# A two-layer hybrid block on one core: the first stage takes its tokens as columns, and two weight sums are made by adding transfers

## The chip, the core and the metric

One core of one Trainium2 chip runs the whole program. The metric is device time in microseconds, the median of three runs. The engines are TensorE (PE; its weight loads are PEld), VectorE (DVE), ScalarE (ACT), GpSimd (POOL) and SyncE (SP, which only issues transfers). Transfers issued by SP or by POOL are carried by the core's 16 DMA engines.

## The reference

256 tokens of width 1024 go through six sublayers, each followed by a residual and a layer norm. Four of them are feed-forward layers (2816 hidden features), one is a mixer of a gated delta rule and a state-space scan (hybrid), one is sparse attention.

```
def swiglu(x, w_in, w_out):
    gate, up = jnp.split(x @ w_in, 2, axis=-1)
    return (jax.nn.silu(gate) * up) @ w_out
...
        h = layer_norm(DEEPNORM_ALPHA * h + 0.5 * swiglu(h, ffn_w_in[layer, 0], ffn_w_out[layer, 0]),
                       ln_g[layer, 0], ln_b[layer, 0])
```

The mixers enter in the same way with the factor 1.

## The kernel before

**Arithmetic.** All arrays are float32. Every factor is split in two, hi (the value rounded to the matmul's format, made by ACT's copy) and lo (the rest, made by DVE as value minus hi), and a product is three matmuls: hi by hi, hi by lo, lo by hi. So each 512 KB weight tile (128 x 1024) is loaded as `raw`, cast by ACT to `whi` and subtracted by DVE to `wlo` (`halved`, line 676), and then used by PE. Tokens stand as columns, `x`, split in the same way; `X` is a copy that isn't split.

**Stages.** The order is feed-forward, hybrid, feed-forward, feed-forward, attention, feed-forward. A feed-forward stage (`ffn`, line 1044) makes its 22 tiles of 128 hidden features in three ways: four by products per block of tokens, two by column products, and the last 16 in four chunks of four by `wide` (line 751). In a chunk the 2 x 2 blocks of w_in (gate and up, two halves of the depth) meet seven combined forms of x (`token_forms`): seven products named a to g, twelve matmuls each, instead of eight. Four weight blocks of two tiles, b11, b12, b21 and b22, are loaded; products b, d, e and f need sums of blocks, which DVE adds in place: b is b11 + b12, d is that + b22, e is b12 + b22, f is (the sum of d) + b21. Each hidden tile then meets a tile of w_out in twelve matmuls (a term) into four PSUM banks, `acc`; `TERMS` says how many terms follow each of a chunk's products. `rows` (line 705) loads the w_out tiles; for the seven in `ADDED` of each stage lo is made by ACT as minus the rounded tile, to which a transfer that POOL issues adds the tile from memory.

**Start.** `run` (line 2103) loads x's rows in four pieces of 256 KB into `h`; PE turns them by transposes against `ident`, and ACT and DVE copy and split the result out of PSUM (`transpose_half`). `first_steps` and `first_weights` (lines 1011 and 717) load the gate and the up tiles, four each, and multiply them with both token blocks. Matmuls of `ones` (`spin`) keep PE at work before and between.

**Order.** The program is recorded and then put in order by a planner (`order`, line 352), which picks for each engine the operation that can start first by its own costs, and by program order among those that can start now. Each engine runs its list in that order and waits at the first operation that isn't ready. All operations carry line 561 in the profile, where the list is written out, so groups are told apart by tile names. SBUF has 52 tiles of 4 KB a partition (`m4`) for all of this.

Of the kernel before, what the change touches and what calls it, by code (L numbers as in the profile page):

```python
# [18 lines left out]
P = 128  # L19
# [3 lines left out]
DFF = 2816  # L23
# [27 lines left out]
CHUNKS, AHEAD, LAG = 4, 3, 7  # L51

TERMS = ((0, 1, 1, 1, 1, 1, 1), (0, 0, 1, 1, 1, 1, 0), (0, 0, 1, 1, 1, 1, 0), (0, 0, 1, 1, 1, 0, 0))

ADDED = range(8, 22, 2)
# [6 lines left out]
RANK = 0  # L62

# [118 lines left out]
class Op:  # L182
    __slots__ = ("eng", "fn", "args", "kw", "idx", "prio", "cost", "table", "deps", "succ", "ndep", "ready", "start",
                 "end", "alloc", "dense", "alts", "tiles", "nbytes", "quad", "port", "banks")


class Plan:
# [11 lines left out]
    def __init__(self):  # L199
        self.ops = []  # L200
        self.tiles = []
        self.base = 0
        self.gate = None
        for e in ("tensor", "vector", "scalar", "gpsimd", "sync"):
            setattr(self, e, _Eng(self, e))
# [7 lines left out]
    def add(self, eng, fn, args, kw, alts=None):  # L213
# [3 lines left out]
        op.alts = alts  # L217
        op.deps, op.succ, op.alloc, op.nbytes = {}, [], None, 0
# [133 lines left out]
    def order(self, caps):  # L352
# [95 lines left out]
        while left:  # L448
            best = None
            for e in engs:  # L450
# [6 lines left out]
                for op in lst:  # L457
# [16 lines left out]
                    key = (st if st > f + 1e-9 else f, p)  # L474
                    if cand is None or key < cand[0]:
                        cand = (key, op, pen)
# [5 lines left out]
            (key, op, pen), e = best  # L482
            st = key[0] + pen
# [101 lines left out]
class K:  # L585
    NT = 2
# [130 lines left out]
    def first_weights(self, w, n0, arrivals):  # L717

        out = []
        for n in range(4):  # L720
            src = w[n0 + n]
            raw = self.m4(1024, "raw", "W")
            hi, lo = (self.m4(1024, name, "W", F32R) for name in ("whi", "wlo"))
            step = 512 if arrivals and n < 2 else 1024
            for e in range(0, 1024, step):
                cs = slice(e, e + step)
                self.nc.sync.dma_start(raw[:, cs], src[:, cs])
                self.split(hi[:, cs], lo[:, cs], raw[:, cs])
                for f in (arrivals.pop(0) if arrivals else []):
                    f()  # L730
            out += [(hi[:, k * 512:k * 512 + 512], lo[:, k * 512:k * 512 + 512]) for k in range(2)]
        return out
# [18 lines left out]
    def wide(self, w, n0, forms, gout):  # L751
# [31 lines left out]
        add(b11, b12)  # L783
# [3 lines left out]
        add(b11, b22)  # L787
        product(r, "d", b11, False, False)
        nc.scalar.activation(t, r, AF.Copy)
        yield  # L790
        add(b12, b22)
# [6 lines left out]
        yield  # L798
        b21 = load(3)
        p = self.bank("ps")  # L800
# [1438 lines left out]
```

## Time and profile before

| | |
|---|---|
| median of three runs | 1086.62 us (1086.55 to 1088.65) |
| the profiled execution's own time | 1087.19 us |
| its span, first to last instruction | 1085.5 us |
| idle time of PE in the span, 1085.5 - 1066.3 | 19.2 us |
| mean DMA rate over the span | 199 GB/s |
| bytes moved | 215.71 MB |
| granted PE clock, mean | 0.995 |

A row of a group reads: line, engine, operation, output <- inputs, sizes, count, then its busy time and the mean of one in ns. A row of the timeline reads: start and length in us, engine, line, operation, and in brackets the idle time before it and what ended it. The granted clock is TensorE's, as a share of full speed.

### The profile page before, as it was taken

What the parts mean: (1) busy time and instruction counts of PE and PEld (TensorE: products, weight loads), DVE (VectorE), ACT (ScalarE), POOL (GpSimd) and SP (SyncE); (2) the same over time, 40 slices, a digit from 0 to 9 for tenths busy, and PEclk for the clock granted to TensorE, in tenths of its full rate; (3) what the DMA queues carried; (4) which work ended last, traced back from release to release, by engine and by line L of the source; (5) the groups of instructions that cost most, each with busy time, mean ns of one, the idle gap of its engine ahead of it and who ended that gap; (6) DMA issues with size and microseconds to landing.
All of it is one profiled execution on the core that took longest, in us unless ns stands there. A gap on an engine that the chain in (4) does not pass through costs nothing.

```text
span 1085.5 us, 16212 instructions
## 1 busy us (share of the span) xinstructions
PE 1066.3 (98%) x5946; PEld 893.3 (82%) x5946; DVE 1010.9 (93%) x1453; ACT 725.9 (67%) x1155; POOL 70.7 (7%) x116
## 2 busy tenths in 40 slices
PE   8999999998999999999999999999999999999997
PEld 6788888897999788888888888888887778888886
DVE  7999999799979999999999999999978889999995
ACT  7767866368737774667866667678465778666780
POOL 1000000001001310000000000000001000000000
PEclk9999999999999999999999999999999899999999
DMA  8658768535433575367777736679563336457881
GB/s 330 231 196 256 221 233 284 179 135 182 140 115 99 194 269 180 117 230 251 215 229 254 257 125 215 235 241 303 189 214 98 92 123 216 152 188 236 255 231 41
DMA packets 65034, 215.71 MB, mean 199 GB/s; under 512 B 8301, under 2 KB 12218, under 8 KB 64954
## 3 DMA queue, kind: packets, MB, share of 16 engines
q1 hardware_dynamic: 60922, 199.98, 52.8%
q0 software_dynamic: 4032, 14.68, 7.2%
q8 instruction: 47, 0.77, 0.3%
q14 instruction: 33, 0.27, 0.1%
HBM read 211.86 MB, written 1.07 MB: 196 GB/s over the span
## 4 chain that ended last, share of the span: by engine, by line
PE 84%; DVE 12%; ACT 1%; DMA 1%; issue 1%; POOL 0%; SPq 0%; DVEq 0%; ACTq 0%
PE ps L561 39%; PE acc L561 31%; PE mp L561 14%; DVE wlo L561 2%; DVE cv L561 2%; DVE arena L561 1%; DMA raw<-in_ffn_w_in_dram 1%; DVE o L561 1%; DVE sw L561 1%; DVE x L561 1%; DVE y L561 1%; DVE qs L561 1%; DVE AT L561 0%; POOL arena L561 0%; DVE Y L561 0%
## 5 line engine op out<-in xcount | busy, mean ns | idle before, releaser
L561 ACT ACTIVATE whi<-raw 128x1024 fp32r<-128x1024 f32 (+1 forms) x435 | 436.8, 1052 | 104.0 <-DVE raw L561 85.4
L561 DVE TENSOR_TENSOR wlo<-raw,whi 128x1024 fp32r<-128x1024 f32 (+2 forms) x419 | 491.4, 1205 | 7.1 <-ACT whi L561 6.1
L561 PE MATMUL ps<-whi,x 128*128 128x512 f32 (+1 forms) x864 | 234.8, 390 | 0.3 <-ACT cv L561 0.3
L561 PEld LDWEIGHTS ps<-whi,x 128*128 128x128 f32 x864 | 156.7, 188 | 30.6 <-issue 1.5
L561 DVE TENSOR_TENSOR raw<-raw,raw 128x1024 f32<-128x1024 f32 x128 | 152.8, 1216 | 0.0
L561 PE MATMUL ps<-wlo,x 128*128 128x512 f32 (+1 forms) x432 | 127.1, 385 | 0.0
L561 PE MATMUL ps<-x,whi 128*128 128x256 f32 (+2 forms) x560 | 114.3, 312 | 4.0 <-ACT cv L561 2.4
L561 PEld LDWEIGHTS ps<-x,whi 128*128 128x128 f32 (+1 forms) x560 | 90.4, 188 | 11.4 <-ACT cv L561 3.8
L561 PE MATMUL acc<-whi,gh 128*128 128x512 f32 x253 | 99.3, 393 | 0.0
L561 PE MATMUL acc<-wlo,gh 128*128 128x512 f32 x253 | 99.0, 391 | 0.0
L561 PE MATMUL acc<-whi,gl 128*128 128x512 f32 x253 | 97.9, 390 | 0.0
L561 PEld LDWEIGHTS ps<-wlo,x 128*128 128x128 f32 x432 | 79.6, 188 | 15.3 <-issue 0.4
L561 PE MATMUL ps<-x,wlo 128*128 128x256 f32 (+1 forms) x344 | 80.0, 284 | 0.5 <-DVE wlo L561 0.5
L561 PE MATMUL acc<-whi,x 128*128 128x512 f32 x224 | 73.7, 405 | 2.3 <-DVE x L561 0.8
L561 PE MATMUL acc<-whi,g 128*128 128x512 f32 x192 | 63.3, 392 | 0.0
L561 POOL DMA_DIRECT2D wlo<-in_ffn_w_out_dram x28 | 24.4, 872 | 569.2 <-ACT wlo L561 391.3
L561 PEld LDWEIGHTS ps<-x,wlo 128*128 128x128 f32 (+1 forms) x344 | 58.1, 189 | 2.1 <-DVE wlo L561 0.7
L561 PEld LDWEIGHTS acc<-whi,gl 128*128 128x128 f32 x253 | 47.5, 188 | 9.8
L561 PEld LDWEIGHTS acc<-whi,gh 128*128 128x128 f32 x253 | 47.5, 188 | 9.5
L561 PEld LDWEIGHTS acc<-wlo,gh 128*128 128x128 f32 x253 | 47.5, 188 | 9.5
L561 PEld LDWEIGHTS acc<-whi,x 128*128 128x128 f32 x224 | 41.8, 189 | 11.8 <-ACT whi L561 2.1
L561 PE MATMUL mp<-whi,fhi 128*128 128x512 f32 x128 | 49.9, 390 | 0.0
(284 smaller groups left out, 1735.2 us busy)
## 6 DMA issues: line engine op xcount, KB each, us to landing
raw<-in_ffn_w_in_dram SPq DMA_DIRECT2D x174, 512.0 KB, 5.5
raw<-in_ffn_w_out_dram SPq DMA_DIRECT2D x88, 512.0 KB, 3.7
wlo<-in_ffn_w_out_dram POOLq DMA_DIRECT2D x28, 512.0 KB, 8.5
raw<-in_hyb_w_col_dram SPq DMA_DIRECT2D x28, 512.0 KB, 4.5
raw<-in_hyb_w_tok_dram SPq DMA_DIRECT2D x16, 512.0 KB, 7.8
raw<-in_hyb_w_out_dram SPq DMA_DIRECT2D x16, 512.0 KB, 3.7
raw<-in_nsa_w_tok_dram SPq DMA_DIRECT2D x8, 512.0 KB, 6.6
raw<-in_nsa_w_one_dram SPq DMA_DIRECT2D x8, 512.0 KB, 5.8
```

The costliest lines, as they stand in the source:

```text
L561: r = getattr(getattr(nc, eng), fn)(*[res(a) for a in args], **{k: res(a) for k, a in kw.items()})
```

## The change

**The start.** The host lays x out a second time as columns (`x_cols`: four pieces of 128 x 512, two depth tiles of both token blocks each). `first_loads` issues these between the weight tiles, straight into `X`, and all 16 transposes and their copies out of PSUM go: ACT and DVE split `X` as it lies in SBUF. The rows of x are still needed for the first residual and are now loaded behind the first stage's weights. The matmuls of `ones` all stand ahead.

```diff
-    def first_weights(self, w, n0, arrivals):
+    def first_loads(self, x, w):
+        raws = []
+        for n in range(8):
+            if n < 4:
+                nc.sync.dma_start(x[1][n // 2][:, :, n % 2 * 2:n % 2 * 2 + 2, :],
+                                  self.i['x_cols'][n].rearrange("p (b k t) -> p b k t", b=2, k=2))
             raw = self.m4(1024, "raw", "W")
+            for cs in [slice(0, 512), slice(512, 1024)] if n == 0 else [slice(0, 1024)]:
+                nc.sync.dma_start(raw[:, cs], w[n][:, cs])
+            raws.append(raw)
+        return raws
...
+                if c0 == 0:
+                    hi, lo = (x[0][n][:, :, e] for e in range(2))
+                    self.split(hi, lo, x[1][n // 2][:, :, n % 2 * 2:n % 2 * 2 + 2, :].rearrange("p b k t -> p k b t"))
...
+            with self.late():
+                nc.sync.dma_start(self.ah[b], self.i['x'][0, b * P:(b + 1) * P])
...
-        spin(4, 2)
+        spin(4, 4)
...
-        load(0, 0)
-        with _Gate(self.plan, len(self.plan.ops) - 3):
-            spin(2, 2)
```

**The sums.** The sums of e and f are made by adding transfers that POOL issues, two tiles each in each of 16 chunks; those of b and d stay on DVE. No w_out tile is made by a transfer any more. Product c moves from the sixth place in a chunk to the second, behind a.

```diff
-ADDED = range(8, 22, 2)
+ADDED, EARLY = (), 3
+SUMS = ("e", "f")
...
-        def add(out, a):
+        def add(name, out, a, block):
             for e in range(2):
-                V.tensor_tensor(out[e], out[e], a[e], OP.add)
+                if name in SUMS:
+                    nc.gpsimd.dma_start(out[e], w[n0 + 2 * block + e], accum_op=OP.add)
+                else:
+                    V.tensor_tensor(out[e], out[e], a[e], OP.add)
...
         b12 = load(1)
-        add(b11, b12)
+        add("b", b11, b12, 1)
+        if "e" in SUMS:
+            add("e", b12, None, 2)
+        b21 = load(3)
+        p = self.bank("ps")
+        product(p, "c", b21, True, True)
...
         product(r, "d", b11, False, False)
+        if "f" in SUMS:
+            add("f", b11, None, 3)
...
-        b21 = load(3)
-        p = self.bank("ps")
-        product(p, "c", b21, True, True)
```

**The planner.** Operations of a layer norm count as able to start 135 ns sooner on DVE and ACT when the next one is picked. Constants for a variant with five chunks come in as well, but all four stages keep four.

```diff
-                    key = (st if st > f + 1e-9 else f, p)
+                    at = st - HOT if op.hot and e in ("vector", "scalar") else st
+                    key = (at if at > f + 1e-9 else f, p)
```

What this makes of the order, at three places. First PE's start. Before (`mp` are transposes, `acc` under 130 the matmuls of ones, `x` the split columns):

```order
L561 MATMUL acc_124<-ones_109 128x512
L561 MATMUL acc_124<-ones_109 128x256
L561 MATMUL mp_143<-ident_126,h_3_111 128x128 x4
L561 MATMUL acc_161<-whi_151,x_157 128x512 x4
L561 MATMUL acc_124<-ones_109 128x256
L561 MATMUL acc_161<-wlo_167,x_157 128x512
L561 MATMUL acc_124<-ones_109 128x256
L561 MATMUL acc_161<-wlo_167,x_157 128x512
L561 MATMUL mp_178<-ident_126,h_5_116 128x128 x4
L561 MATMUL mp_183<-ident_126,h_3_111 128x128 x4
L561 MATMUL acc_191<-whi_151,x_157 128x512 x3
L561 MATMUL mp_206<-ident_126,h_5_116 128x128 x4
```

And PE's start now:

```order
L569 MATMUL acc_128<-ones_109 128x512 x2
L569 MATMUL acc_168<-whi_163,x_157 128x512 x2
L569 MATMUL acc_172<-whi_163,x_157 128x512 x2
L569 MATMUL acc_168<-whi_163,x_157 128x512 x2
L569 MATMUL acc_172<-whi_163,x_157 128x512 x2
L569 MATMUL acc_168<-wlo_166,x_157 128x512 x2
L569 MATMUL acc_172<-wlo_166,x_157 128x512 x2
L569 MATMUL acc_168<-whi_187,x_177 128x512 x4
```

The transposes and the later matmuls of ones are gone, and the last row is the first product of weight tile 1, which stood behind all four groups of transposes.

Second SP's start, before (`h` are x's rows):

```order
L561 DMA h_3_111<-in_x_dram 128x512
L561 DMA raw_113<-in_ffn_w_in_dram 128x512 x2
L561 DMA h_5_116<-in_x_dram 128x512
L561 DMA h_3_111<-in_x_dram 128x512
L561 DMA h_5_116<-in_x_dram 128x512
L561 DMA raw_153<-in_ffn_w_in_dram 128x512 x2
```

And now (`X` are x's columns; up to `h` the first stage's loads, behind it the next weights):

```order
L569 DMA X_3_111<-in_x_cols_dram 128x2x256
L569 DMA raw_113<-in_ffn_w_in_dram 128x512 x2
L569 DMA X_3_111<-in_x_cols_dram 128x2x256
L569 DMA raw_119<-in_ffn_w_in_dram 128x1024
L569 DMA X_8_123<-in_x_cols_dram 128x2x256
L569 DMA raw_125<-in_ffn_w_in_dram 128x1024
L569 DMA X_8_123<-in_x_cols_dram 128x2x256
L569 DMA raw_130<-in_ffn_w_in_dram 128x1024
L569 DMA raw_134<-in_ffn_w_in_dram 128x1024
```

Weight tile 1 (`raw_119` now, `raw_153` before) stands behind two pieces of x instead of four; later four more weight tiles and then `h` follow.

Third DVE in the first chunk, before, from the sum of b on (`raw<-raw,raw` are the sums; 407 and 409 are b11's tiles, 438 and 440 b12's):

```order
L561 TENSOR_TENSOR raw_407<-raw_407,raw_438 128x1024
L561 TENSOR_TENSOR raw_409<-raw_409,raw_440 128x1024
L561 TENSOR_TENSOR sg_478<-ps_466,sg_478 128x256
L561 TENSOR_TENSOR wlo_523<-raw_407,whi_512 128x1024
L561 TENSOR_TENSOR sg_478<-sg_478 128x256
L561 TENSOR_TENSOR sg_534<-ps_503,sg_534 128x256
L561 TENSOR_TENSOR raw_407<-raw_407,raw_540 128x1024
```

And now, from the split of d to that of f (455 and 457 are b11's tiles; between its first and its last row here the adding transfer for f into `raw_455` has to land):

```order
L569 TENSOR_TENSOR wlo_623<-raw_455,whi_611 128x1024
L569 TENSOR_TENSOR wlo_637<-raw_457,whi_626 128x1024
L569 TENSOR_TENSOR wlo_647<-raw_628,whi_634 128x1024
L569 TENSOR_TENSOR wlo_659<-raw_512,whi_643 128x1024
L569 TENSOR_TENSOR wlo_670<-raw_514,whi_653 128x1024
L569 TENSOR_TENSOR wlo_679<-raw_655,whi_667 128x1024
L569 TENSOR_TENSOR wlo_690<-raw_577,whi_675 128x1024
L569 TENSOR_TENSOR wlo_699<-raw_579,whi_683 128x1024
L569 TENSOR_TENSOR vg_702<-mp_584,vg_702 128x512
L569 TENSOR_TENSOR wlo_714<-raw_685,whi_693 128x1024
L569 TENSOR_TENSOR wlo_725<-raw_455,whi_707 128x1024
```

There are nine rows between the first and the last, all splits but one. Of the sums, rows like the first two of before, DVE keeps those of b and d.

More of the change, by code (lines that the diff above doesn't have):

```diff
@@ L62 @@
 RANK = 0
+HOT = 135.0
 HARD = False
@@ L183 @@
     __slots__ = ("eng", "fn", "args", "kw", "idx", "prio", "cost", "table", "deps", "succ", "ndep", "ready", "start",
-                 "end", "alloc", "dense", "alts", "tiles", "nbytes", "quad", "port", "banks")
+                 "end", "alloc", "dense", "alts", "tiles", "nbytes", "quad", "port", "banks", "hot")
 class Plan:
@@ L715, in rows, with first_weights @@
         return hi, lo
-    def first_weights(self, w, n0, arrivals):
-        out = []
-        for n in range(4):
-            src = w[n0 + n]
-            raw = self.m4(1024, "raw", "W")
[L723 to L732, printed above, removed]
+    def first_loads(self, x, w):
+        nc = self.nc
+        raws = []
[3 more added lines that the diff above has]
+                                  self.i['x_cols'][n].rearrange("p (b k t) -> p b k t", b=2, k=2))
+            raw = self.m4(1024, "raw", "W")
+            for cs in [slice(0, 512), slice(512, 1024)] if n == 0 else [slice(0, 1024)]:
+                nc.sync.dma_start(raw[:, cs], w[n][:, cs])
+            raws.append(raw)
+        return raws
+    def first_weights(self, raw, parts):
+        hi, lo = (self.m4(1024, name, "W", F32R) for name in ("whi", "wlo"))
+        for cs in parts:
+            self.split(hi[:, cs], lo[:, cs], raw[:, cs])
+        return [(hi[:, k * 512:k * 512 + 512], lo[:, k * 512:k * 512 + 512]) for k in range(2)]
     def token_forms(self, x):
@@ L938, in ln_params, with layer_norm, normalize @@
         return g, bb
-    def layer_norm(self, b, acc, s, gb, x, last):
+    def layer_norm(self, *args):
+        self.plan.hot = True
+        self.normalize(*args)
+        self.plan.hot = False
+    def normalize(self, b, acc, s, gb, x, last):
         nc, V = self.nc, self.nc.vector
@@ L1091, in ffn @@
                 self.scale_h(b)
-        terms, late, wos = [], [], []
+        terms, late, wos = [], [], {}
         def weights_to(n):
-            while len(wos) < min(n, NF):
-                wos.append(self.rows(w_out, len(wos), len(wos) in ADDED))
+            for f in range(NF):
+                if f not in wos and f < n + EARLY * (f in ADDED):
+                    wos[f] = self.rows(w_out, f, f in ADDED)
         def flush(most):
@@ L1107, in ffn @@
         terms += [(f, gts[f]) for f in range(2 * NT)]
-        steps = NF // 2 - 2 * CHUNKS
+        steps = NF // 2 - 2 * CH
+        if steps == NT:
+            forms = self.token_forms(x)
         for s in range(NT, steps):
-            wg, wu = (self.col_tiles([w_in[8 + 4 * (s - NT) + 2 * n + e] for e in range(2)]) for n in range(2))
+            wg, wu = (self.col_tiles([w_in[4 * NT + 4 * (s - NT) + 2 * n + e] for e in range(2)]) for n in range(2))
             self.mark = len(self.plan.ops) - 1
@@ L1124, in ffn @@
         weights_to(AHEAD)
-        for n in range(CHUNKS):
+        for n in range(CH):
             f0 = 2 * steps + 4 * n
             gout = [self.m4(1024, name, "G", F32R).rearrange("p (f t) -> p f t", f=4) for name in ("gh", "gl")]
-            part = self.wide(w_in, 8 + 4 * (steps - NT) + 8 * n, forms, gout)
-            for most in TERMS[n]:
+            part = self.wide(w_in, 4 * NT + 4 * (steps - NT) + 8 * n, forms, gout)
+            for most in TERMS[CH][n]:
                 next(part)
@@ L2194, in laid_out @@
             else:
-                t = [rows(np.concatenate([g[:, c:c + 256], u[:, c:c + 256]], 1), 2) for c in (0, 256)]
+                t = [rows(np.concatenate([g[:, c:c + 256], u[:, c:c + 256]], 1), 2) for c in ((0, 256) if CH < 5 else (0,))]
             for c in range(512, steps * 256, 256):
```

52 lines of the change are left out of this document (29 added, 23 removed).

## The prediction

> **What bounds the kernel now.** I read the page's first part first.
>
> ```profile
> PE 1066.3 (98%) x5946; PEld 893.3 (82%) x5946; DVE 1010.9 (93%) x1453; ACT 725.9 (67%) x1155; POOL 70.7 (7%) x116
> ```
>
> Both PE and DVE look full; which of them sets the pace where the change works? The change works in two places: the first 50 us, and the chunks of the four feed-forward stages. For the chunks I asked for the busy time in stretches that lie inside them, one in each stage, and ahead of these in two stretches of the start (stretch, length, each engine's busy time and instructions, granted clock, the DMA engines' busy share, GB/s).
>
> ```profile
> 2.00:9.00 7.00, 5.50 (x18) 3.39 (x16) 2.71 (x6) 2.04 (x5) 2.12 (x11) 1.00 0.90 285
> 10.00:23.00 13.00, 12.24 (x56) 9.73 (x55) 11.83 (x17) 12.57 (x21) 0.00 (x0) 1.00 1.03 415
> 54.00:162.00 108.00, 108.00 (x489) 89.38 (x488) 107.15 (x105) 78.27 (x92) 5.34 (x6) 1.00 0.71 227
> 459.00:594.00 135.00, 135.00 (x613) 111.49 (x612) 132.05 (x137) 94.15 (x112) 7.02 (x8) 1.00 0.74 238
> 648.00:756.00 108.00, 108.00 (x489) 89.42 (x488) 106.53 (x123) 76.72 (x92) 6.02 (x7) 1.00 0.75 243
> 945.00:1053.00 108.00, 108.00 (x489) 89.31 (x488) 107.63 (x106) 79.92 (x94) 5.25 (x6) 1.00 0.72 223
> ```
>
> PE is busy throughout, and three stages give the very same 489 matmuls in 108 us. DVE is at 98 to 99%. A busy PE is modelled, so I checked with the chain of waits, by line, for 54 to 162 us.
>
> ```profile
> by line: PE ps L561 43.0%; PE acc L561 38.5%; PE mp L561 18.8%
> ```
>
> No step of DVE, ACT or DMA is in it: in the chunks PE's own matmuls are the whole chain, and DVE, though full, keeps up. What DVE is spared there gives back no time by itself. The start is different. This is its chain (start, length, what):
>
> ```profile
> 1.73 4.92 DMA raw<-in_ffn_w_in_dram
> ...
> 9.88 0.60 ACT X L561
> ...
> 11.06 0.44 DVE x L561
> ...
> 12.71 8.89 PE acc L561 x39
> 21.60 7.27 PE ps L561 x32
> ...
> 29.37 7.09 DMA raw<-in_ffn_w_in_dram
> ```
>
> Up to 12.7 us the chain goes through a load, the transposes and the copies of x out of PSUM; then PE works without a break (32 matmuls in 7.27 us, 0.227 each) until about 32. So the start has time to win, and the rest has little.
>
> **The change part by part.** *Start.* Rows of before's timeline (start, length, engine, operation, idle time before it):
>
> ```profile
> 1.06 2.93 PE L561 MATMUL acc<-ones 128*128 128x512 f32 x4 [1.06 <-POOL ones L561]
> ...
> 3.79 1.06 PE L561 MATMUL mp<-ident,h 128*128 128x128 f32 x4
> ...
> 9.24 1.03 PE L561 MATMUL mp<-ident,h 128*128 128x128 f32 x8
> ...
> 13.24 2.01 PE L561 MATMUL acc<-whi,x 128*128 128x512 f32 x8
> ...
> 13.94 6.81 ACT L561 ACTIVATE whi<-raw 128x1024 fp32r<-128x1024 f32 x7
> ```
>
> Weight tile 1's products start at 13.24, and 84 matmuls follow back to back. When can they start in the changed kernel? There they need x's first two pieces (256 KB each) and weight tiles 0 and 1 (512 KB each): 1.5 MB. Before's first six loads are 1.5 MB too, and the sixth is the last of x's four:
>
> ```profile
> L561 SPq DMA_DIRECT2D h<-in_x_dram x4: 393/432/432, 0.8 to 3.1; - x4
> DMA to landing us min/median/max: 2.5/5.2/5.5
> ```
>
> Issued at 3.1 with at most 5.5 to landing, it is there at 8.6 us. The new order brings the same bytes, but x's rows now land in two runs of 1 KB where before's were one of 2 KB. No row has such runs. If they cost nothing, tile 1 is there at 8.6; if a run of 1 KB takes as long as one of 2 KB, the two pieces take their time once more, 0.5 MB at the 285 GB/s of 2 to 9 us, 1.8 us, and it is there at 10.4. I take 9.1, nearer the first, since the other loads keep their form. ACT's cast of tile 1 follows (7 in 6.81 us, 1.0 each) with 0.2 us for signals: start at 10.3, bounds 9.8 and 11.6. Against 13.24 that is **-2.9 us (-3.4 to -1.6)**. Later tiles keep ahead: 12 matmuls take 2.7 us, and their 768 KB land in 1.9 us at the 415 GB/s of 10 to 23 us. The 16 transposes are inside this term, all before 13.24.
>
> *Behind the first products* PE waits for DVE to empty the two PSUM banks:
>
> ```profile
> 28.91 3.33 SPq L561 DMA_DIRECT2D raw<-in_ffn_w_in_dram x6
> ...
> 30.49 2.35 DVE L561 TENSOR_TENSOR flo<-X,fhi 128x1024 fp32r<-128x1024 f32 x2
> ...
> 32.76 1.28 DVE L561 TENSOR_TENSOR sg<-ps,sg 128x512 f32<-128x512 f32 x2
> ...
> 33.59 2.08 PE L561 MATMUL ps<-x,whi 128*128 128x512 f32 x8 [1.11 <-DVE sg L561]
> ```
>
> The two flo splits hold up sg. In the changed kernel x's pieces and so flo come early; what stays is the multiplication itself, half of 1.28 us. Saved: **-0.5 us** (0 to -0.6).
>
> *The first chunk's weights* are late already: SP issues them from 28.91, and the chain row above has the second landing at 29.37 + 7.09 = 36.5 us. Now SP issues the token rows of x (1 MB) ahead of them, 2.5 us at 415 GB/s, while PE wants them 3.4 us sooner. Before's first use is this row:
>
> ```profile
> 46.46 1.09 PE L561 MATMUL ps<-whi,x 128*128 128x512 f32 x4
> ```
>
> So 10 us of cover become 4. Products c and a of the new order need two tiles more, at 1.3 us each, and the casts: the cover is about gone. PE's new order has eight matmuls of w_out between a and c to fill in. **+0.4 us** (0 to +2.5).
>
> *Transfers for sums.* On DVE, 64 of these additions go, and 28 of the second kind come back since no w_out tile is made by transfer any more:
>
> ```profile
> L561 DVE TENSOR_TENSOR wlo<-raw,whi 128x1024 fp32r<-128x1024 f32 (+2 forms) x419 | 491.4, 1205 | 7.1 <-ACT whi L561 6.1
> ...
> L561 DVE TENSOR_TENSOR raw<-raw,raw 128x1024 f32<-128x1024 f32 x128 | 152.8, 1216 | 0.0
> ```
>
> 64 x 1.216 - 28 x 1.205 = 44 us less on DVE, 2.7 us in each of 16 chunks; on PE's chain that is **0**. What it costs is transfers. Before's 28 adding transfers:
>
> ```profile
> q0 software_dynamic: 4032, 14.68, 7.2%
> ```
>
> That is 0.072 x 1085.5 / 28 = 2.8 us of all DMA engines each. In the 108 us of the first stretch 14 replace 6: 22 us more, so the share goes from 0.71 to 0.92, under the 1.03 that 10 to 23 us held. Loads still come in time on average: **0**. How long one takes to land, from POOL's issue:
>
> ```profile
> L561 POOL DMA_DIRECT2D wlo<-in_ffn_w_out_dram x28: 844/862/1046, 88.2 to 1053.5; - x28
> DMA to landing us min/median/max: 5.4/8.5/11.2
> ```
>
> Sum f is the tighter one. Between DVE's last read of its tile (wlo of d) and the next (wlo of f) stand some nine DVE rows, eight of 1.2 us and one of 0.7: 10.4 us, less ACT's cast, 9.4. A landing after 8.5 is in time, one after 11.2 is 1.8 late. ACT waits for it in its queue, with casts for later products behind it, and DVE behind ACT. But 1.8 is under the 2.7 us that DVE was spared, so PE need not notice. On POOL only the adding transfers themselves queue in the chunks (0.9 us each); its layer norm step comes after the last of a stage.
>
> *Products c first, layer norm's operations first (135 ns in the planner):* PE's waits in the whole run, longest first:
>
> ```profile
> PE ps L561 <- ACT cv L561: 2.7, 3, 1.3
> PE ps L561 <- DVE sg L561: 1.6, 2, 1.1
> ```
>
> None at a layer norm is longer, since a stage's last terms cover it: **0** (-0.5 to +0.5). The hybrid and attention stages keep their order but for their first and last rows.
>
> Sum: -2.9 - 0.5 + 0.4 = **-3.0 us**. The profiled execution took 1087.19 us, 1.7 around its span of 1085.5 which the change leaves alone; it lies 0.6 over the median of 1086.62. So 1084.2 as it was profiled, and **1083.6** against the median.
>
> **The rivals.** *The sums land late (slower).* With both tiles' transfers in flight beside loads, f's second one can wait for the first: 11.2 + 2.8 = 14 us at worst. Up to 9.4 + 2.7 = 12.1 us DVE's relief pays; at 13 each chunk loses 0.9 us if no split is ahead of PE, 16 x 0.9 = 14: 1086.6 - 3.0 + 14 = 1098. For it: the transfers more than double, and the share rises to 0.92. Against it: the longest of 28 was 11.2, and PE never waited for a split in the chunks. [...]
>
> *PE is cold when the products start.* Four transposes at 3.79 took 1.06 us, eight at 9.24 took 1.03: PE ran at half speed before. Before has PE work of ones placed in the gaps; now all of it stands at the beginning, and from about 4.8 to 10.3 PE has only 12 matmuls. If it falls back, the products from 10.3 on run at half speed for as long as the slow rows last here, 1.06 to 4.85 us, and half of these 3.8 us is given back: 1083.6 + 1.9 = 1085.5. Against it: before's own gaps were about as long. [...]
>
> *The gain is given back at the first chunk.* If its weights are 2.5 us late, and the last term is +2.5: -2.9 - 0.5 + 2.5, 1085.7.
>
> **How the numbers follow.** A measurement of this kernel can tell about 0.2%, 2.2 us, from no change. My forecast gets 0.63, the cold PE 0.12, the first chunk 0.10, the late sums 0.15. The forecast's own bounds run from -4.5 (3.4 + 0.6 + 0.5) to about -1.2, 1082.1 to 1085.4; some 0.55 of it all lies below -2.2 us. The two middle rivals and the forecast's upper end are within 0.2%: 0.30. The late sums are slower: 0.15. The range from 1081.3, a little under the lowest sum, to 1089.0, into the mild part of the late sums, leaves out about 0.2.
>
> **What would show it.** Right: tile 1's products start near 10.3 us and the row of 32 ps matmuls near 18.7; PE's wait behind it is near 0.6; the chunk stretches again hold 489 matmuls in 108 us with PE as their whole chain, while DVE falls to about 90% and the DMA share rises above 0.9. Wrong: ACT rows whi waiting for DMA raw inside chunks with PE waits behind them (late sums); 0.45 us a matmul after 10 us (cold); the gain seen at 30 us gone at 60 (first chunk).

## The result, and the profile after

The changed kernel takes **1098.65 us** (median of 1098.22, 1098.65 and 1102.2), the kernel before 1087.05 beside it: ratio **1.0114, 95% interval 1.0085 to 1.0142**. It is slower by over 1%, where 1083.6 was forecast. (A fourth run, 1180 us at a clock of 0.848, is left out, as every comparison here leaves such runs out.) The profiled execution took 1098.22, its span is 1096.5, 11.0 more than before's.

First the start, where the change did what it says. PE's timeline of the changed kernel (start, length, operation, in brackets the idle time before):

```profile
10.66 1.67 PE L569 MATMUL acc<-whi,x 128*128 128x512 f32 x6 [1.34 <-ACT whi L569]
...
19.00 1.98 PE L569 MATMUL ps<-whi,x 128*128 128x512 f32 x8
...
30.46 0.48 PE L569 MATMUL ps<-x,whi 128*128 128x512 f32 x1 [0.42 <-DVE sg L569]
...
42.58 1.09 PE L569 MATMUL ps<-whi,x 128*128 128x512 f32 x4
```

Weight tile 1's products start at 10.66 (13.24 before), PE is back behind the first products at 30.46 (33.59), and the first chunk begins at 42.58 (46.46) without a wait. At 43 us the change is 3.9 us ahead. Now the stretches inside the chunks that were shown of before (length, busy time of PE, PEld, DVE, ACT, POOL with counts, granted clock, DMA share, GB/s):

```profile
54.00:162.00 108.00, 103.64 (x465) 84.50 (x465) 100.68 (x98) 74.54 (x86) 12.05 (x14) 1.00 0.88 258
459.00:594.00 135.00, 133.30 (x608) 110.05 (x607) 120.79 (x123) 90.71 (x108) 12.12 (x14) 1.00 0.88 264
648.00:756.00 108.00, 108.00 (x489) 89.03 (x487) 99.36 (x113) 73.37 (x87) 10.26 (x12) 1.00 0.91 269
945.00:1053.00 108.00, 108.00 (x492) 89.34 (x491) 103.16 (x105) 75.35 (x90) 12.20 (x14) 1.00 0.89 260
```

DVE is relieved and the DMA share is near the 0.92 that was forecast, but the first stage's chunks hold 465 matmuls where 489 ran before: 24 x 108 / 489 = 5.3 us lost, more than the start won. The later stages lose at the last chunk, outside the two stretches that still read 108. PE's waits in the whole run (sum, times, longest):

```profile
PE ps L569 <- ACT vg L569: 6.2, 4, 1.6
PE mp L569 <- DVE vg L569: 5.4, 5, 1.6
PE acc L569 <- ACT whi L569: 2.8, 3, 1.3
PE ps L569 <- ACT cv L569: 2.7, 3, 1.7
```

The first two lines are new: nine waits, 11.6 us, for `vg`, all in the chunks. Seven of them, 8.7 us, wait for an operation that empties a PSUM bank (in `wide`, ACT's copy of bank r after product e, and DVE's subtraction from bank q). The other two, 1.27 us at 109.95 and 1.58 at 145.16, wait for a product of DVE that PE then turns by transposes. In the chunks PE waits neither for a transfer nor for a split; the third line is casts at the start, before 54 us. Yet the chain of 54 to 162 us, in before made of PE alone, now leads through transfers (by line, and then its first piece):

```profile
by line: DMA raw<-in_ffn_w_in_dram 11.0%; DMA raw<-in_ffn_w_out_dram 7.4%; DVE wlo L569 5.1%; PE ps L569 3.8%; PE mp L569 3.1%; PE acc L569 2.5%; issue 2.2%; DVE vg L569 1.8%; DVE raw L569 1.1%; ACT whi L569 1.0%; DVEq L569 0.1%
...
121.15 11.87 DMA raw<-in_ffn_w_in_dram
```

The 7.4% is a load that is still under way at the stretch's end, so it says nothing. The 11.0% is this one piece, an adding transfer of POOL's; behind it the chain goes through ACT's cast and DVE's splits to the second of the two waits for a product, at 145.16.

One of the nine places shows how the two hang together. Timeline of the changed kernel at the last chunk of the second feed-forward stage, rows of POOL, ACT, DVE and PE:

```profile
565.47 0.88 POOL L569 DMA_DIRECT2D raw<-in_ffn_w_in_dram  x1 [1.57 <-DVE wlo L569]
...
571.29 0.60 ACT L569 ACTIVATE su<-ps 128x512 f32<-128x512 f32 x1 [1.04 <-PE ps L569]
575.03 3.90 ACT L569 ACTIVATE whi<-raw 128x1024 fp32r<-128x1024 f32 x4 [3.14 <-DMA raw<-in_ffn_w_in_dram]
578.83 0.57 ACT L569 ACTIVATE vg<-ps 128x512 f32<-128x512 f32 x1
...
576.12 4.63 DVE L569 TENSOR_TENSOR wlo<-raw,whi 128x1024 fp32r<-128x1024 f32 x4 [3.15 <-ACT whi L569]
580.67 0.68 DVE L569 TENSOR_TENSOR vg<-mp,vg 128x512 f32<-128x512 f32 x1
...
576.08 0.62 PE L569 MATMUL ps<-wlo,fhi 128*128 128x512 f32 x2
...
577.66 0.39 PE L569 MATMUL acc<-whi,gl 128*128 128x512 f32 x1
579.46 1.20 PE L569 MATMUL ps<-whi,x 128*128 128x512 f32 x4 [1.41 <-ACT vg L569]
...
581.41 0.50 PE L569 MATMUL mp<-whi,fhi 128*128 128x512 f32 x1 [0.29 <-DVE vg L569]
```

POOL issues f's second transfer at 565.47. ACT is ready for its cast at 571.89, 6.4 us later, and gets the tile at 575.03. Behind this cast stand three more, and behind these the copy of bank r after product e. PE finishes what it has at about 577.9 and wants to add product f onto bank r, which must be copied first: it waits until 579.46. The same on DVE: four splits, late by 3.15 us, stand ahead of `vg`, for which product g's bank waits at 581.41. The last chunk of every feed-forward stage has such a wait for ACT's copy (165.80, 579.46, 757.65 and 1060.91 us, 1.4 to 1.6 us each), each behind a cast for which ACT idled 3.1 to 3.4 us.

ACT takes its queue in order here: product e's last two matmuls (576.08 for 0.62 us) end at 576.70, and the copy starts at 578.83, 2.13 us later, behind the four casts that stand ahead of it (575.03 for 3.90 us).

### The profile page after: what moved, and what is told of

The parts are those of the page before. It is cut to its first block, busy times and chain, and to the rows that moved or that the text cites. A ratio compares the mean times of both kernels' runs of the same rounds, so it can differ in the third digit from the quotient of the medians.

```text
span 1096.5 us, 16191 instructions
## 1 busy us (share of the span) xinstructions
PE 1066.2 (97%) x5926; PEld 889.0 (81%) x5926; DVE 976.2 (89%) x1411; ACT 699.0 (64%) x1119; POOL 100.5 (9%) x152
## 4 chain that ended last, share of the span: by engine, by line
PE 69%; DVE 10%; DMA 5%; issue 2%; ACT 1%; POOL 1%; DVEq 0%; POOLq 0%; ACTq 0%
PE ps L569 33%; PE acc L569 25%; PE mp L569 12%; DMA raw<-in_ffn_w_in_dram 5%; DVE wlo L569 3%; DVE arena L569 1%; DVE cv L569 1%; ACT whi L569 1%; DMA raw<-in_ffn_w_out_dram 1%; POOL arena L569 1%; DVE qs L569 0%; DVE sw L569 0%; DVE vg L569 0%; DVE x L569 0%; DVE AT L569 0%
## 5 line engine op out<-in xcount | busy, mean ns | idle before, releaser
L569 DVE TENSOR_TENSOR wlo<-raw,whi 128x1024 fp32r<-128x1024 f32 (+2 forms) x446 | 522.3, 1209 | 37.3 <-ACT whi L569 34.3
L569 ACT ACTIVATE whi<-raw 128x1024 fp32r<-128x1024 f32 (+2 forms) x430 | 428.9, 1049 | 72.4 <-DMA raw<-in_ffn_w_in_dram 41.7
L569 POOL DMA_DIRECT2D raw<-in_ffn_w_in_dram x64 | 55.6, 868 | 497.6 <-DVE raw L569 154.6
L569 DVE TENSOR_TENSOR raw<-raw,raw 128x1024 f32<-128x1024 f32 x64 | 76.3, 1215 | 0.0
L569 ACT ACTIVATE su<-ps 128x512 f32<-128x512 f32 x48 | 28.4, 593 | 66.2 <-PE ps L569 59.4
```

Source lines behind the costliest of these rows:

```text
L569: r = getattr(getattr(nc, eng), fn)(*[res(a) for a in args], **{k: res(a) for k, a in kw.items()})
```

## The experiments

The theories. **L**: the sums' transfers land too late. **B**: product c in second place needs a PSUM bank at once, and that alone makes PE wait. **Load**: the transfers slow everything by their share of the DMA engines. **Q**, formed later: a late tile costs only where the emptying of a bank stands behind its cast in ACT's or DVE's queue. In all kernels `SUMS`, `ADDED` and `HOT` are the constants shown with the change. `TERMS` is the list of w_out terms; the change also sets one of its entries from 1 to 0, so that one term of a stage's first chunk is held back, and the prediction has no term for that.

The table has every kernel with its median, its ratio to the kernel before with the 95% interval, and PE's gaps in the profiled execution: distances between starts of successive matmuls beyond the usual one of their form, in us, summed over four stretches (0 to 54; 54 to 189, the first stage's chunks; 189 to 405, the hybrid stage; 405 to 783 and 918 to the end, the other feed-forward stages). The attention stage has 29.5 to 31.0 in all but the start with the changed term list, 32.4.

| kernel | us | ratio | 0-54 | 54-189 | hybrid | other ffn |
|---|---|---|---|---|---|---|
| before | 1087 to 1088 | | 9.0 | 1.2 | 30.4 | 4.0 |
| changed | 1098.65 | 1.0114 [1.0085, 1.0142] | 6.8 | 8.1 | 30.5 | 11.5 |
| plain loads | 1083.68 | 0.9961 [0.9948, 0.9973] | 6.3 | 1.1 | 30.4 | 4.3 |
| planner told 1.5 | 1091.28 | 1.0042 [1.0025, 1.0059] | 6.0 | 5.5 | 30.9 | 6.7 |
| planner told 3.0 | 1085.27 | 0.9979 [0.9970, 0.9987] | 6.6 | 1.8 | 31.8 | 4.6 |
| only e by transfer | 1090.97 | 1.0034 [1.0021, 1.0048] | 6.0 | 1.5 | 34.3 | 6.4 |
| only f by transfer | 1093.62 | 1.0053 [1.0041, 1.0065] | 6.5 | 5.5 | 30.5 | 10.1 |
| c fourth | 1089.11 | 1.0013 [1.0004, 1.0021] | 6.2 | 1.8 | 35.4 | 5.1 |
| c fourth, told 3.0 | 1089.29 | 1.0018 [1.0010, 1.0027] | 7.1 | 2.4 | 34.1 | 4.9 |
| c sixth | 1096.72 | 1.0081 [1.0064, 1.0099] | 6.7 | 6.9 | 31.2 | 6.4 |
| c sixth, only e | 1100.67 | 1.0114 [1.0097, 1.0131] | 6.8 | 16.0 | 31.1 | 7.7 |
| c sixth, told 3.0 | 1093.51 | 1.0051 [1.0038, 1.0064] | 6.4 | 2.7 | 34.5 | 8.1 |
| sums on DVE, c second | 1101.53 | 1.0128 [1.0114, 1.0142] | 6.7 | 7.2 | 35.6 | 9.9 |
| start, changed term list | 1120.67 | 1.0304 [1.0281, 1.0327] | 8.6 | 9.9 | 38.4 | 15.8 |
| start, term list of before | 1093.67 | 1.0049 [1.0034, 1.0064] | 5.8 | 7.4 | 32.1 | 4.3 |
| start, told 3.0 | 1095.16 | 1.0064 [1.0051, 1.0076] | 6.8 | 6.7 | 34.6 | 4.9 |
| before, told 3.0 | 1088.91 | 1.0007 [0.9997, 1.0017] | 9.9 | 1.2 | 30.5 | 4.5 |
| told 3.0, old start | 1090.00 | 1.0022 [1.0013, 1.0030] | 8.5 | 1.2 | 30.4 | 7.4 |
| told 3.0, no head start | 1090.65 | 1.0020 [1.0012, 1.0029] | 6.6 | 2.7 | 34.5 | 4.1 |
| term back | 1102.52 | 1.0134 [1.0120, 1.0148] | 6.2 | 6.8 | 30.5 | 14.4 |

The four columns read by stage where the loss sits: for the changed kernel 6.9 us in the first stage's chunks and 7.5 in the other three feed-forward stages, against 2.1 won at the start.

### Is it the adding transfers?

```diff
-                    nc.gpsimd.dma_start(out[e], w[n0 + 2 * block + e], accum_op=OP.add)
+                    nc.gpsimd.dma_start(out[e], w[n0 + 2 * block + e])
```

> The changed kernel, order and all, with the 64 adding transfers made plain loads from the same places into the same tiles: the sums of e and f are left out (their products get one block alone). A plain load reads 512 KB where an adding one took all DMA engines 2.8 us or so; if it takes half of that and lands 3 us sooner, theory L (late landing) expects ACT's waits for DMA in the chunks to fall from 42 us to under 15 and the time to 1084 to 1088. Theory B (order, c in second place, a bank held) expects 1095 to 1098 still, since nothing of the order changes.

1083.68 us, ratio 0.9961 [0.9948, 0.9973]. ACT's waits for w_in's transfers fall from 41.7 to 17.8 us, a little less than expected. The software queue's line of this kernel (packets, MB, share of 16 engines), and then the landing of POOL's 64 transfers:

```profile
q0 software_dynamic: 9216, 33.56, 8.9%
```

```profile
DMA to landing us min/median/max: 3.7/5.2/8.2
```

And the same two of the changed kernel, with the same packets and bytes:

```profile
q0 software_dynamic: 9216, 33.56, 17.0%
```

```profile
DMA to landing us min/median/max: 5.4/7.9/11.9
```

So one adding transfer of 512 KB takes all engines 0.170 x 1096.5 / 64 = 2.9 us and a plain one 0.089 x 1081.2 / 64 = 1.5. At the place shown above ACT's timeline now reads:

```profile
563.43 0.60 ACT L569 ACTIVATE su<-ps 128x512 f32<-128x512 f32 x1 [1.04 <-PE ps L569]
564.87 3.91 ACT L569 ACTIVATE whi<-raw 128x1024 fp32r<-128x1024 f32 x4 [0.83 <-DMA raw<-in_ffn_w_in_dram]
568.87 0.60 ACT L569 ACTIVATE vg<-ps 128x512 f32<-128x512 f32 x1
```

The same rows in the same order, with 0.83 us of waiting in place of 3.14, and no PE wait behind them. Theory B falls as the whole cause: PE, ACT, DVE and POOL run the same lists in the same order through the whole trace. This kernel leaves sums out, so it is a measurement and no repair; in it all the rest of the change (start, DVE's relief, c second, head start) is worth -4.3 us of span, 1081.2 against 1085.5. But plain loads are both sooner and lighter, so L and Load are not told apart.

### Landing, load or order in the queue?

The planner takes an adding transfer to land 0.6 us after its bytes have passed. Both kernels move that alone; transfers and program stay.

```diff
-                op.end = at + 600
+                op.end = at + (3600 if e == 'gpsimd' else 600)
```

> The changed kernel, its transfers and its program as they are; only the planner is told that an adding transfer lands 1.5 us later than it assumed. It then puts other work ahead of the casts that wait for one. Theory Q (a late landing costs because in ACT's and DVE's queues the emptying of PSUM banks stands behind the casts of f) expects much of the loss gone: 1085 to 1092, with PE's waits for vg under 5 us in sum (11.6 in the changed kernel). If the transfers cost by their load on the DMA engines, 1095 to 1099 as before.

> The same with 3.0 us, past the longest landing seen (11.9 us). Theory Q expects 1083 to 1088, near the version whose transfers are plain loads (1083.7). If the load counts, 1095 to 1099.

1091.28 us, ratio 1.0042 [1.0025, 1.0059], with 1.5 us (2100 in the line; PE's waits for vg fall from 11.6 to 5.3 us, where under 5 was expected), and 1085.27, 0.9979 [0.9970, 0.9987], with 3.0. In the second, the transfers are as heavy as ever (queue's line) and land hardly sooner (POOL's 64):

```profile
q0 software_dynamic: 9216, 33.56, 17.3%
```

```profile
DMA to landing us min/median/max: 5.2/7.6/10.6
```

ACT's longest wait for DMA in that kernel, and then PE's three longest waits of all:

```profile
ACT whi L569 <- DMA raw<-in_ffn_w_in_dram: 37.1, 41, 3.0
```

```profile
PE ps L569 <- ACT cv L569: 2.7, 3, 1.2
PE acc L569 <- ACT whi L569: 2.3, 3, 1.1
PE mp L569 <- ACT P L569: 1.2, 1, 1.2
```

ACT still waits for DMA 37.1 us in sum (41.7 in the changed kernel), up to 3.0 at a time, and PE never waits for vg. ACT's timeline at the same chunk shows why:

```profile
566.63 1.06 ACT L569 ACTIVATE whi<-raw 128x1024 fp32r<-128x1024 f32 x1 [0.23 <-DMA raw<-in_ffn_w_in_dram]
571.19 0.60 ACT L569 ACTIVATE vg<-ps 128x512 f32<-128x512 f32 x1 [3.49 <-PE ps L569]
571.68 2.94 ACT L569 ACTIVATE whi<-raw 128x1024 fp32r<-128x1024 f32 x3
```

The copy of bank r now stands ahead of the casts. The stretches are those that the prediction asked for:

```profile
54.00:162.00 108.00, 108.00 (x488) 89.03 (x487) 99.91 (x98) 74.70 (x87) 12.08 (x14) 1.00 0.91 266
...
945.00:1053.00 108.00, 108.00 (x489) 89.42 (x489) 99.82 (x99) 74.44 (x88) 10.48 (x12) 1.00 0.91 268
```

488 and 489 matmuls in 108 us, DVE at 92%, DMA share 0.91. Load falls, L in its plain form too: neither the share nor ACT's waits are the price. What they hold up in the queue is. Theory Q stands, and this version beats both kernels, the one before by 0.2%. That is clear of the noise between runs, but no larger than what the order of another stage is worth in some of the kernels below.

### Which sum, and how long a cover

Both edits leave the transfers of one sum and put the other on DVE: `SUMS = ("e",)` and `SUMS = ("f",)`.

> The changed kernel with the sums of f back on DVE; e's stay transfers, w_out has none. DMA transfers for sums fall from 64 to 32, DVE gets 32 x 1.2 = 39 us back, so it is about as full as in the kernel before. If it is f's transfers that land late (they have the short cover of 9 us, e's have three products), ACT's waits for DMA fall by half or more and the time is 1083 to 1087. If it is the load of 64 transfers on the DMA engines as such, about half of the loss stays: 1089 to 1093. If DVE was needed as free as the change made it, 1093 or more.

> The changed kernel with e's sums back on DVE; f's stay transfers, 32 of them. If f's short cover is the cause, ACT still waits for f's tiles and PE for vg: 1094 to 1099, near the changed kernel and 3 us or more above the version with only e's (1091.0). If the number of transfers is the cause, it comes out like that one, 1089 to 1093.

1090.97 us, ratio 1.0034 [1.0021, 1.0048], with e's transfers; 1093.62, 1.0053 [1.0041, 1.0065], with f's. Both medians lie outside the ranges expected if f is the cause, and the first lies in the one for the load of the transfers. They are close, since the first carries 34.3 us of gaps in the hybrid stage. In the feed-forward stages it is clear: 1.5 + 6.4 against 5.5 + 10.1, where the kernel before has 1.2 + 4.0 and the changed one 8.1 + 11.5. Of the 14.4 us that these stages lost, f's transfers alone keep 10.4 and e's 2.7. ACT's waits for w_in's transfers are 40.7 us with f's and 19.1 with e's. With c second it is f, the sum with the short cover.

Product c moved behind d, so that two more splits stand between d's last read and f:

```diff
-        b21 = load(3)
-        p = self.bank("ps")
-        product(p, "c", b21, True, True)
...
         nc.scalar.activation(t, r, AF.Copy)
         yield
+        b21 = load(3)
+        p = self.bank("ps")
+        product(p, "c", b21, True, True)
```

> The changed kernel with product c moved from second to fourth place, behind d: f's transfers can then start two splits of DVE (2.4 us) sooner before f is due, all transfers kept. Theory L expects ACT's waits for DMA in the chunks to shrink (each by up to 2.4 us; 41.7 us in the whole run before) and the time to fall to 1085 to 1090. If the load on the DMA engines is the cause, it stays at 1095 to 1099.

> The version with c in fourth place (1089.1 us) with the planner told 3.0 us. If cover and number do the same thing, nothing is added beyond the orders of the hybrid stage, whose PE gaps came out as 30 to 32 us in some kernels and 34 to 35 in others: 1084 to 1089. Chunk gaps should stay as small as before this edit.

1089.11 us, ratio 1.0013 [1.0004, 1.0021], and with the planner told as well 1089.29, 1.0018 [1.0010, 1.0027], just above the range. ACT's waits in the first:

```profile
ACT whi L569 <- DMA raw<-in_ffn_w_in_dram: 7.6, 14, 1.3
```

From 41.7 to 7.6 us, with all 64 adding transfers kept, and the chunk gaps go (1.8 and 5.1 us). ACT's waits for DVE's sums rise from 24.3 to 74.1 us in their place, and they hold PE up as little as its waits in the told version did. Told and cover add nothing to each other. What keeps both near 1089 is the hybrid stage with 34 to 35 us of gaps; in all eight kernels of the table with 34 us or more one wait is a good part of the difference, in the first of these two:

```profile
PE mp L569 <- DVE y L569: 2.3, 1, 2.3
```

The change and these edits touch next to nothing in that stage; the planner's order there comes out one way or the other. What decides it was not tried.

### Product c's place

Product c back in sixth place, the rest as changed; then with e's transfers alone; then with the planner told.

```diff
-        product(p, "c", b21, True, True)
...
         V.tensor_tensor(u, q, t, OP.subtract)
+        yield
+        b21 = load(3)
+        p = self.bank("ps")
+        product(p, "c", b21, True, True)
```

> The changed kernel with product c back in sixth place; the sums of e and f stay with POOL's transfers. Theory L expects it to stay slow, 1094 to 1100, since the late sums stand in ACT's and DVE's queues as before. Theory B expects PE's waits for vg ahead of ps matmuls (6.2 us in the changed kernel) to go and the time to fall to about 1087 or below.

> The changed kernel with f's sums back on DVE and product c back in sixth place; e's sums stay transfers. Theory LB (the loss needs both: f's late transfer delays ACT's queue, and c in second place has PE wait for what stands in it) expects this at or under the version with f's sums alone taken back (1091.0), 1084 to 1090, and no PE wait over 1.2 us in the chunks. If c in sixth place costs by itself (waits for su), it comes out above 1091.

> The repaired version (sums by transfer, planner told 3.0 us) with product c back in sixth place. If c in second place is what lets the sums be hidden, PE waits for su again and the time is 1088 to 1094; if its place does not matter once the planner is told, 1084 to 1087.

1096.72 us (1092.39 to 1098.82, ratio 1.0081 [1.0064, 1.0099]; its profile is the fastest of these), 1100.67 (1.0114 [1.0097, 1.0131]) and 1093.51 (1.0051 [1.0038, 1.0064]). The waits for vg go, but others come: in the first two PE waits for `su`, here the copy of bank r after product d. PE's waits for it in the second kernel, and then ACT's rows at the longest:

```profile
PE ps L569 <- ACT su L569: 9.8, 5, 3.6
```

```profile
95.70 1.06 ACT L569 ACTIVATE whi<-raw 128x1024 fp32r<-128x1024 f32 x1 [2.59 <-DMA raw<-in_ffn_w_in_dram]
96.66 0.58 ACT L569 ACTIVATE su<-ps 128x512 f32<-128x512 f32 x1
```

It is Q's pattern again, now with sum e: its second transfer is issued at 84.32 and lands at 95.62, ACT's cast waits for it, and the copy of bank r stands right behind that cast. The four longest of these waits (58.84, 97.29, 133.50 and 168.31 us) all have such a cast ahead, for which ACT waited 1.5 to 3.1 us. With c sixth, product c no longer lies between e's transfer and its use, so e's cover is the short one. This is what c's second place is worth: with it, e's transfers cost little. My expectation for the second (1084 to 1090) missed, so "late f and c second together" was wrong as a theory. With the planner told, PE has no wait for `su` left, though the time lies where it was expected with one. Here c second is better than sixth by 4.4 us of gaps in the feed-forward stages (1.8 + 4.6 against 2.7 + 8.1), and what makes these gaps was not found.

The sums on DVE with c second and the transfers for w_out (`SUMS = ()`, `ADDED, EARLY = range(8, 22, 2), 0`):

> The changed kernel with all sums on DVE and the seven adding transfers for w_out as before; product c stays in second place, and the head start of 135 ns stays. Theory L (the sums' transfers land late, ACT waits for them in its queue, and the evacuations behind them come late) expects the loss gone: 1083 to 1085. Theory B (c in second place needs the PSUM bank of the chunk before at once, and that alone makes PE wait for ACT) expects most of it kept, 9 to 16 waits of PE for vg of 1 to 2 us: 1093 to 1098. A mixture would lie between.

1101.53 us, ratio 1.0128 [1.0114, 1.0142]. Neither expectation holds: PE waits 6.2 us for the adding transfers of w_out, and 1.1 for vg. The term list of the changed kernel is in it, so it does not isolate c's place.

### Why not the start alone?

The changed start in the kernel before; first with the changed term list, second with `TERMS` of before, third with the planner told as well, and beside them the kernel before with only the planner told.

```diff
-SUMS = ("e", "f")
+SUMS = ()
-ADDED, EARLY = (), 3
+ADDED, EARLY = range(8, 22, 2), 0
-HOT = 135.0
+HOT = 0.0
-TERMS = {4: ((0, 0, 1, 1, 1, 1, 1)
+TERMS = {4: ((0, 1, 1, 1, 1, 1, 1)
```

> Only the new start is kept: all sums on DVE, seven w_out tiles a stage by adding transfers as before, product c in sixth place, no head start for layer norm's operations. Every theory that puts the loss into the chunks expects the start's gain to show: tile 1's products at 10.7 us, PE back behind the first products at about 30.5, and 3 us under the kernel before, 1083 to 1084.5. If instead the new start itself spoils the first stage (x's rows and the earlier PE meeting late weights), the first stage's layer norm comes as late as in the changed kernel or later, and the time is that of the kernel before or above, 1087 to 1090.

> The new start alone once more, now with the list of w_out terms of the kernel before: one term follows the second product of a stage's first chunk, which the changed kernel holds back to the stage's end. Everything in the chunks is then as before. If the term held back made the 33 us of the earlier run (its last w_out tiles by transfer then come late), the time is 1083 to 1085, the 3 us that the start saves. If that run was slow for the start itself, it stays at 1110 to 1121.

> The new start with the term list of before (the run that came out 0.5% slower than the kernel before), and the planner told that an adding transfer, here the 28 for w_out, lands 3.0 us later. Theory Q for the start (it loses because w_out's adding transfers then come late for PE in the first stage) expects the start's 3 to 4 us to show at last: 1083 to 1086, no wait of PE for DMA wlo. If the start itself costs, 1090 to 1095 again.

> The kernel before with the same number told to its planner. PE never waited for a transfer or a split in its chunks, so theory Q expects no gain: 1086 to 1090. A gain of 2 us or more would say that the 1085.3 us of the repaired version is not owed to the change.

1120.67 us (1.0304 [1.0281, 1.0327]), 1093.67 (1.0049 [1.0034, 1.0064]), 1095.16 (1.0064 [1.0051, 1.0076]) and 1088.91 (1.0007 [0.9997, 1.0017]). The first two lie outside all the ranges that were expected of them. Two things come out. The one w_out term that the changed list holds back costs 27 us where w_out's adding transfers are kept. And the start alone does not win at all: it leads at 30 us and loses 5.5 to 8.7 us in the first stage's chunks. In the third kernel PE no longer waits for a w_out tile by transfer, as theory Q asked, and the loss stays. Where is it? Of this kernel, DVE and PE in the second chunk:

```profile
92.32 5.87 DVE L569 TENSOR_TENSOR wlo<-raw,whi 128x1024 fp32r<-128x1024 f32 x5 [0.56 <-ACT whi L569]
98.11 0.68 DVE L569 TENSOR_TENSOR vg<-mp,vg 128x512 f32<-128x512 f32 x1
...
98.84 0.50 PE L569 MATMUL mp<-whi,fhi 128*128 128x512 f32 x1 [2.02 <-DVE vg L569]
```

And its stretches:

```profile
54.00:162.00 108.00, 105.17 (x471) 85.44 (x469) 106.75 (x104) 76.18 (x91) 4.64 (x6) 1.00 0.69 216
162.00:180.00 18.00, 17.23 (x80) 14.16 (x80) 18.00 (x20) 14.90 (x19) 1.56 (x2) 1.00 1.04 337
```

DVE is full to the last (18.00 of 18.00 us), and PE, 3 us early, waits for a bank that DVE empties behind five splits. In the second kernel PE waits 1.9 us at 97.6 us for a w_out tile by adding transfer instead. It is tempting to say that the start can bring nothing while DVE has 107 us of work in 108. The version with only e's sums by transfer speaks against it. It has the new start too, and these are its stretches:

```profile
54.00:162.00 108.00, 108.00 (x489) 89.28 (x489) 106.60 (x105) 72.82 (x86) 5.19 (x6) 1.00 0.78 234
162.00:180.00 18.00, 18.00 (x85) 14.92 (x84) 17.81 (x23) 15.06 (x17) 0.79 (x1) 1.00 0.67 256
```

Its DVE is as full, 124.4 us of 126 against 124.75, and PE loses nothing: 489 matmuls in 108 us. So a full DVE is not enough to lose the start's gain. The two kernels differ in e's sums, c's place, w_out's adding transfers, the term list, the head start and the planner's number. The start with c second, all sums on DVE and no adding transfer was not run. Which of these keeps the gain is therefore not shown. Telling the planner gains nothing in the kernel before, so that number alone does not make the 1085.27.

The counterpart, the told version with the start of before:

```diff
-        raws = self.first_loads(x, w_in)
+            w = self.first_weights(w_in, 4 if c0 else 0, arrivals)
```

> The repaired version (1085.3 us: sums by transfer, c second, planner told 3.0 us) with the start of the kernel before in it, transposes and all. If the new start is worth its 3 us there, this is 1087.5 to 1089.5, and PE is back behind the first products at 33.5 us in place of 30.2. If the gain of the repaired version is owed to the sums, it is 1084 to 1086.

1090.00 us, ratio 1.0022 [1.0013, 1.0030], just above the range: 4.7 above the told version, 3.5 by the profiled spans (1088.1 and 1084.6). Of these, 1.9 are gaps at the start, and 1.9 are matmul time in place of gaps (the span's difference less that of all gaps, 77.0 and 75.4), the transposes and PE's slow rows there (in the kernel before, two matmuls take 1.06 us at 5.46 and 0.63 at 12.77); the other stages cancel out to -0.3. PE is back behind the first products at 32.98 in place of 30.16. In the told version the start is worth 2.8 us there and 3.5 to 4.7 by the whole time; 3.4 were forecast for its first two terms.

### Two small constants

> The changed kernel with one number of its list of w_out terms set back: one term follows the second product of a stage's first chunk again, as in the kernel before. If holding that term to the stage's end costs in the changed kernel (as the two runs of the start alone suggest for transfers of w_out), the time falls to 1088 to 1093. Theory L (late sums) expects 1095 to 1100 still.

> The repaired version without the head start of 135 ns for layer norm's operations. The prediction put that at 0 (-0.5 to +0.5): 1084.5 to 1086.5 expected. More than 1 us either way, in the trace at the layer norms or in the hybrid stage, would show that term wrong.

The term set back in the changed kernel (`TERMS` as in the diff above): 1102.52 us, ratio 1.0134 [1.0120, 1.0148], no gain, so the held-back term is not where the changed kernel loses. Without the head start (`HOT = 0.0`) the told version takes 1090.65, 1.0020 [1.0012, 1.0029], where 1084.5 to 1086.5 was expected. By the profiled spans it loses 2.8 us (1087.4 against 1084.6), and gaps in the hybrid stage are 2.7 us longer, with the same wait for y of 2.3 us. By the sign that was named beforehand, the prediction's 0 for the head start was wrong here, by way of the hybrid stage's order and not at layer norms.

## Why the prediction was wrong

- **Start, -2.9 us: right.** 10.66 against the 10.3 forecast, -2.6 us, inside the bounds; the row of 32 ps matmuls at 19.0 against 18.7. The 0.2 us for signals in the forecast was an estimate that no run shows: tile 1, issued at 3.26, landed 6.3 us later, its cast ran from 9.55 to 10.61, and the products began 0.05 us behind it.
- **Wait behind the first products, -0.5: right** but for its bound of -0.6: 0.42 us in place of 1.11, -0.7.
- **First chunk's weights, +0.4: not paid.** PE begins it 3.9 us sooner without a wait. The rival that gives the gain back there did not come.
- **PE cold at the start: did not come.** The row of eight matmuls at 19.00 takes 1.98 us, 0.23 from start to start, and the six at 10.66 (1.67 us) stand 0.26 apart in the mean, where half speed, twice the usual 0.227, would be 0.45. The granted clock reads 1.00 from 5.0 to 12.4 us. It also reads 1.00 from 3.7 to 5.0 us in the kernel before, so the half speed that the prediction read from two rows of transposes there was its author's estimate.
- **Sums by transfer, 0: the step that failed.** It measured +15 us (span 1096.5 against 1081.2 with plain loads). The share (0.92 forecast, 0.88 to 0.91), the 2.9 us of each transfer and the landing over all 64 (5.4 to 11.9 us, median 7.9, against 5.4 to 11.2 and 8.5) were sized well. Three other parts of the step were wrong. The tile: 8.5 was taken, but f's second tiles, for which ACT waits, landed after 6.5 to 11.9 us, in the median 9.45. The cover: nine DVE rows, 9.4 us, were counted on DVE and for one chunk's first tile; the cast of f's second tile came up on ACT 6.4 us after its issue, so a landing after 9.5 was 3.1 late, not 0.1. And the sentence "1.8 is under the 2.7 us that DVE was spared, so PE need not notice" asked when PE gets its next split. In the chunks PE did not wait for one. It waited for copies and subtractions out of PSUM, and twice for a product, that stood behind late casts and splits. DVE's relief does nothing for ACT's queue, and DVE itself stood idle for ACT's casts, 34.3 us ahead of its splits where the kernel before has 6.1:

```profile
L569 DVE TENSOR_TENSOR wlo<-raw,whi 128x1024 fp32r<-128x1024 f32 (+2 forms) x446 | 522.3, 1209 | 37.3 <-ACT whi L569 34.3
```

The told version shows it: the same relief, nearly the same waits of ACT (37.1 us in place of 41.7), no wait of PE for vg.

- **The rival "late sums"** had the time, 1098, and 0.15 of the chance. Its sign came, casts waiting for transfers with PE waits behind them. But its working was as wrong as the cover: it needed a second landing past 12.1 us and 0.9 us lost in each of 16 chunks, and none landed later than 11.9 and PE lost its time at nine places. That its 1098 is the measured time is luck.
- **"What DVE is spared gives back no time by itself"**: true of the chunks before. Beside the new start it stays open: alone the start lost 0.5%, while the version with only e's sums by transfer kept it with DVE as full.
- **c second and the head start, 0:** nothing of these shows in the changed kernel (its hybrid stage has 30.5 us of gaps, 30.4 before). With the planner told, c second was worth 4.4 us of gaps against sixth. The bounds of half a microsecond were too tight: in eight of these kernels the hybrid stage has 3.7 to 8.0 us more of gaps than before.

Are the sums' transfers late because POOL issues them, beside a busy DVE? With plain loads POOL's 64 transfers landed after 5.2 us in the median, beside a DVE that is busy for 90% of the span; SP's w_in loads of that kernel took 5.8. In that comparison the issue by POOL costs nothing; the adding itself does, with 7.9 us in the changed kernel, where DVE is busy for 89%.

## What to carry to other kernels

When a producer becomes slower, look in each in-order queue that waits for it at what stands behind the waiting instruction: the price was set here by the emptying of a bank or another hand-back there, not by the late tile's own use (with the planner told, PE never waited for vg while ACT still waited 37.1 us), and telling the order's planner a longer time to landing won it back (1098.65 to 1085.27 us) with the same transfers. Count a cover on the engine that waits first, for the last of the tiles in flight, in more than one stage. A gain at the start can be lost again in the very next stage: test each part alone and the whole without it, as both can differ from the sum, and look for a kernel that contradicts the cause before naming it.

## What the runs showed of the hardware

An adding transfer costs about twice a plain one: 2.9 against 1.5 us of all 16 engines for 512 KB, and 7.9 against 5.2 us to landing in the median, at the same packets and bytes and in the same order of the program.

A wait of PE can cost more than itself. In the kernel with c sixth and e's transfers alone PE's timeline behind its longest wait, and the stretch that follows it (length, busy times, granted clock third from the end), read:

```profile
97.29 0.65 PE L569 MATMUL ps<-whi,fhi 128*128 128x512 f32 x1 [3.59 <-ACT su L569]
97.75 0.63 PE L569 MATMUL ps<-whi,flo 128*128 128x512 f32 x1
98.17 0.63 PE L569 MATMUL ps<-whi,fhi 128*128 128x512 f32 x1
```

```profile
97.20:100.80 3.60, 3.51 (x9) 2.73 (x10) 3.40 (x4) 3.60 (x5) 0.00 (x0) 0.54 0.19 25
```

After 3.59 us of idling the granted clock is 0.54 in this stretch, and eight matmuls start 0.43 us apart where 0.227 is usual: 1.6 us more on top of the wait. From 90.0 to 93.5 us it was 1.00, and from 100.8 to 104.0 it is 0.99. Not every long wait is followed by this: the kernel with c sixth and both sums by transfer waits 2.97 us (to 93.01) and keeps 1.00 over 54 to 162 us. Over the whole profiled execution the clock is 0.991 in the kernel with e's transfers alone and 0.997 in the other. The one stretch shown costs 3.6 x 0.46 = 1.7 us of full clock, 0.0015 of the span of 1100.6 us, so it is not the whole difference. Which waits are followed by a slow stretch, and why, was not tested. The waits for vg of up to 1.6 us in the changed kernel have no such rows behind them: the granted clock behind the four for ACT's copy (165.7 to 170.0, 579.4 to 583.0, 757.6 to 762.0 and 1060.9 to 1065.0 us) reads 1.00.
